# A gate sum moved from the first feed-forward into the mixer of a float32 decoder trunk

## The chip, the cores and the metric

The kernel runs on one core of a Trainium2 chip. TensorE (PE) multiplies matrices, VectorE (DVE) and ScalarE (ACT) work on tiles in on-chip memory, GpSimd (POOL) does little here, and SyncE (SP) issues nearly all transfers from HBM. The engines run beside one another and each takes its own instructions in program order. The metric is the device time of one execution in microseconds (us); "step" below always means one step of the adaLN sums described further on.

## The reference, cut to what matters

Two layers, each made of three sub-layers: a half-step SwiGLU feed-forward, a mixer of three attention branches, and another half-step feed-forward. Every sub-layer has a shift, a scale and a gate, each 1024 wide, that come from the conditioning vector `c`:

```python
mod = (jax.nn.silu(c) @ w_ada[l] + b_ada[l]).reshape(Bn, 3, 3, D_MODEL)
def pre(xx, j):
    return rmsnorm(xx, norm_gain[l, j]) * (1 + mod[:, j, 1]) + mod[:, j, 0]
h = pre(x, 0); x = x + 0.5 * mod[:, 0, 2] * swiglu(h, gate[l, 0], up[l, 0], down[l, 0])
h = pre(x, 1); x = x + mod[:, 1, 2] * (merged(h) @ w_out[l])
h = pre(x, 2); x = x + 0.5 * mod[:, 2, 2] * swiglu(h, gate[l, 1], up[l, 1], down[l, 1])
```

The batch is 1, there are 256 tokens of width 1024, the feed-forward is 2816 wide, and everything is float32. `w_ada` holds 9216 columns per layer, 75 MB in all. The shift and scale of a sub-layer are needed at its norm; its gate is needed only at its end, when the residual is added.

## The kernel before

The sub-layers are numbered s = 0 to 5; s = 1 and s = 4 are mixers. Weights stream through in units of 128 x 1024 numbers. A load (`raw`, 1 MB, three buffers, `load_raws`) holds two units. `feed` (lines 137 to 160) splits each unit into a high part wH (a cast on ScalarE, line 149) and a low part wL (a subtraction on VectorE, line 157), up to five units ahead of the products, with six slots. TensorE then makes three products for each pair of blocks: high with high, low with high, high with low. `step` (line 564) handles one unit: `feed`, `ada_tick`, the unit's products, then whatever follows them.

The adaLN sums run beside this. A sum (s, kind), kind 0 for shift, 1 for scale, 2 for gate, takes eight steps, one for each block of 128 rows of `w_ada`. A step loads 128 x 1024 numbers (512 KB, tag `ada`, two buffers, `ada_load`, line 255), multiplies them by 128 numbers of silu(c) and adds them to the sum's tile `acc` (three buffers). The first step of a sum (kb 0) is on ScalarE (line 280), the other seven on VectorE (line 282). The load of step i + 2 is issued on SP when step i has freed its buffer. Steps go in one fixed order: (0, 2), (1, 0), (1, 1), (1, 2), (2, 0) and so on; steps 16 to 23 are the gate of s = 0, steps 40 to 47 the gate of s = 1.

When a sum is complete, `ada_reduce` (line 326) adds its 128 partitions on TensorE. For a gate that is a product of ones with `acc` in two halves (line 343, tile `adag`, four instructions) and two additions of the bias on VectorE (line 348). For a shift or scale it is a product (line 352, tile `adam`), a copy, transposes and a small evacuation. The dictionary `filler` (line 179) names the sums that are reduced in the gap after a sub-layer, while the next norm runs; every other sum is put on the list `soon` when its eighth step is issued and is reduced five ticks later.

The pace of the steps is set by hand. In `run` (from line 1291) each sub-layer gets the number `need` of steps that are due by its end, plus `SPARE`; `need` is spread over its ticks in proportion to `PACE[s]`. For s = 0 there are 50 ticks left at that point: 8, 8 and 16 gate and up units and 18 of the 22 down units. For s = 1 the parts are 6 value units (pace 0), 14 query and key units, branches of 10, 10 and 12 units, and 4 of the 8 output units. `ada_tick` adds the pace to a credit and issues a step for each whole 1 in it.

`run_rows` (line 703) ends a sub-layer. The body multiplies one unit of 128 rows at a time for all 256 tokens. The last four units (`TAIL`) go piece by piece instead: all four for the first tokens' first 512 columns, then for the next piece, so that residual, norm and transposes (line 487, tile `psn`) of the first tokens run beside the rest. After s = 0 `v_early` (line 938) puts the first value products of the mixer into the gap.

In the mixer (`run_mixer`) the attention stages are placed by hand behind certain units (dictionary `when`): for example the stick-breaking sums (tile `pc`, line 984) behind query unit 9, which need `e` from VectorE (line 978), and the transposes of the second dilated group (tile `pt_dil`, line 1100) behind unit 6 of the first branch, which need that group's scaled probabilities from VectorE (line 1081).

Of the kernel before, what the change touches and what calls it, by code (L numbers as in the profile page):

```python
# [28 lines left out]

# slots of split units, how many of them are split ahead, and slots of loads  # L30
NB = 6
AHEAD = 5
RAWS = 3
# units at the end of a sub-layer whose products go piece by piece, and those that the first norm's transposes follow
TAIL = 4
LEAD = 1
HALVES = ((0, 512), (512, 512))
# columns of the sums that the last rows' products take at a time, by token block
PIECES = (HALVES, ((0, 512), (512, 256), (768, 256)))
# the first shift and scale, by quarter after the first: row blocks on the vector engine, the pass that the rest follows  # L40
FIRST_DVE = (2, 3, 3)
HOOK = (0, 1, 1)
# reductions before the last tokens' transposes, by sub-layer; the others follow
N1 = (1, 3, 3, 2, 1, 0)
# steps of adaLN: how they spread over the parts of each sub-layer, steps beyond what is due, units until a reduction
START_PACE = 0.3
PACE = ((1, 0.75, 1, 1.5), (0, 1.5, 1.5, 1, 0.75, 0.75), (2, 1.5, 1, 1), (1, 0.5, 1, 0.75), (1, 2, 0, 0, 1, 2),
        (1, 1, 1, 1))
SPARE = 1
SOON = 5  # L50
# the last rows' columns on the vector engine; the activation engine takes the others
CUT = 640
# [10 lines left out]
def shape_constants():  # L63
    """One-hot of the bucket of each distance, and the mask of each head by distance (distance 255 - index)."""
    dist = 255 - np.arange(NDIST)
    ok = dist >= 0
    b = _buckets()
    onehot = np.zeros((32, NDIST), np.float32)
    onehot[b[dist[ok]], np.arange(NDIST)[ok]] = 1.0
    mask = np.full((NHEAD, NDIST), NEG, np.float32)  # L70
    for h in range(NHEAD):
        if h < 6:
            w, d = ((128, 1), (512, 4), (2048, 16))[h // 2]
            keep = ok & (dist % d == 0) & (dist // d <= w // d)
        else:
            keep = ok & (dist <= 127)
        mask[h, keep] = 0.0
    return onehot, mask


class Unit:
    """A piece of a weight: `view` picks it from the raw tile of load `raw`; `pe` runs its products."""

# [5 lines left out]
class Trunk:  # L89
# [22 lines left out]

    # ---------------------------------------------------------------- weight stream
    def add_raw(self, loads, small=False):
# [22 lines left out]
    def feed(self, ahead=AHEAD, high=0):  # L137
        """Split the units that lie up to `ahead` in front of the products, H one step before L."""
        self.load_raws()
# [24 lines left out]

    # ---------------------------------------------------------------- adaLN
    def ada_setup(self):
        first = [(0, 0), (0, 1)]
        rest = [(0, 2), (1, 0), (1, 1)]
        for s in range(1, 6):
            rest += [(s, 2)] + ([(s + 1, 0), (s + 1, 1)] if s < 5 else [])  # L170
        self.ada_order = first + rest
        self.ada_pos = 0
        self.ada_kb = 0
        self.ada_acc = {}
        self.ada_raw = []
        self.ada_loaded = 16
        self.gate = {}
        # after which sub-layer a sum is reduced, while the next norm runs; the others as they are complete
        self.filler = {(1, 2): 0, (2, 2): 1, (3, 0): 1, (3, 1): 1, (3, 2): 2, (4, 0): 2, (4, 1): 2, (4, 2): 3,
                       (5, 0): 3, (5, 2): 4}  # L180
        self.credit = 0.0
        self.pace, self.ticks = [0.0], 0
        self.soon = []

    def first_load(self, q):
        """Two blocks of columns of the first shift and scale, into what the feed-forward takes later."""
        t = self.sp.tile([P, KB, 2, 256], F32, tag=("bigA", "bigB")[q % 2], name=f"first{q}", bufs=1)
        for kb in range(KB):
            src = self.a["w_ada"][0, kb * P:(kb + 1) * P, 0:2 * D].rearrange("p (c n) -> p c n", c=2)
            self.nc.sync.dma_start(t[:, kb], src[:, :, 256 * q:256 * q + 256])  # L190
        self.first_src[q] = t

    def first_mac(self, q, kbs):
        """Products of some blocks of rows with the vector, on the vector engine."""
        for kb in kbs:
# [8 lines left out]
    def first_sum(self, q, kbs, acc=False):  # L204
        """Sums over the rows, of products made here or before: a column tile each for the two blocks of the shift
        and of the scale."""
        for kb in ([None] if acc else []) + list(kbs):
# [21 lines left out]
    def first_h(self, q, xt, out):  # L229
        """The first norm's output, two blocks of features."""  # L230
        for i in range(2):
# [94 lines left out]
    def ada_reduce(self, ch):  # L326
        """Sums over the partitions on the tensor engine; returns what is left to do.

        A gate is wanted along the free dimension: ones times the products. Shift and scale are wanted along the
        partitions: four column tiles sum a quarter of the columns each, and transposes turn the rows."""  # L330
        nc = self.nc
# [37 lines left out]

    # ---------------------------------------------------------------- constants  # L370
    def constants(self):
# [67 lines left out]

    # ---------------------------------------------------------------- norm  # L440
    def square(self, t, cols, tag):
        """Mean square over some of the columns."""
        nc = self.nc
# [36 lines left out]
    def norm_pe(self, t, s, xn):  # L480
        """Features to the partitions, one half of them a bank."""
        ps = []
# [8 lines left out]
    def norm_evac(self, t, s, ps, between=()):  # L491
        """Scale and shift by feature, one engine a bank; the high parts too."""
        nc = self.nc
# [46 lines left out]
    def final_gain(self, t, sl):  # L540
        """x times the gain, while the mean square is summed."""
        self.o[t] = self.o.get(t) or self.work([P, D], f"o{t}")
# [19 lines left out]

    # ---------------------------------------------------------------- unit lists
    def step(self, u):
# [15 lines left out]
    def aform(self, u, out, xh, xl, off=0, part="all"):  # L580
        """out += W^T x for one block of 128 columns of the unit; the products with the low part of x come last."""
        nc = self.nc
# [8 lines left out]
    def col_raw(self, src, widths=((0, 256),)):  # L591
        """Load of columns of a [1024, n] weight as [128, 8, 256]."""
        loads = []
# [7 lines left out]
    def plan_ffn(self, l, i, s):  # L601
# [5 lines left out]
        def start_pe(b0, q):  # L607
            """Two blocks of columns over two of rows; both sums of a block share a bank."""
            def pe(u, between=None):
# [74 lines left out]
    def plan_rows(self, w, nk):  # L684
        """Units of one block of 128 rows of a [n, 1024] weight, two a load."""
        us = []
# [9 lines left out]
    def bform(self, u, kb, t, cols, out, xh, xl, first, last):  # L696
        """out += x[t]^T W for one block of rows and some of the columns."""
        sl = slice(t * P, (t + 1) * P)
# [4 lines left out]
    def run_rows(self, us, s, xh, xl, early=None):  # L703
        """Row units to token-major sums, the residual and the next norm.

        The last units' products go piece by piece, so that the norm of the first tokens runs beside them."""
        n = len(us)
# [101 lines left out]

    # ---------------------------------------------------------------- mixer  # L810
    def plan_mixer(self, l, s):
# [125 lines left out]
    def v_early(self, plan):  # L937
        """The first tokens' products with the value columns that are split by now."""
        s = plan["s"]
# [8 lines left out]
    def sb_stages(self, s):  # L948
        """Two heads at a time, keys on the partitions."""
        nc = self.nc  # L950
# [60 lines left out]
    def soft_stages(self, s, l):  # L1011
# [92 lines left out]
        def pv(o, cols, pairs):  # L1104
            """Heads of both halves of the partitions beside one another."""
            n = len(pairs)
# [83 lines left out]
    def run(self):  # L1190
# [100 lines left out]
        for n, plan in enumerate(plans):  # L1291
            s = plan["s"]
            # enough steps of the coming sums for what this sub-layer and the gap behind it reduce
            due = [i for i, (j, kind) in enumerate(self.ada_order)
                   if self.filler.get((j, kind), j - (kind < 2)) <= s]
            need = 8 * (max(due) + 1) - self.ada_pos + SPARE
            if plan["kind"] == "mix":
# [45 lines left out]
```

## Time and profile before

| what | value |
|---|---|
| median of 3 runs | 1215.85 us (1215.71 to 1215.98) |
| profiled execution, span from first to last instruction | 1213.2 us |
| TensorE busy | 1184.2 us, 98% of the span |
| VectorE busy | 830.4 us, 68% |
| ScalarE busy | 615.6 us, 51% |
| transfers | 287.58 MB, mean 237 GB/s |
| mean granted TensorE clock | 0.994 |

The profile tells the span of one execution; the device time has a little more around it, 2.65 us here against the median. The page's share of busy time is a mean over stages that have different limits, so what counts is who ends each wait, stage by stage. Times in the rows are us from the start of the span. In a timeline row the first number is the start, the second the duration, and a bracket tells how long the engine sat idle before it and what released it.

### The profile page before, as it was taken

To read this page: it belongs to the slowest core of one execution; us is meant where nothing else is said; L and a number is where in the kernel's file an instruction comes from. 1 tells how busy PE (TensorE), PEld (TensorE's weight loads), DVE (VectorE), ACT (ScalarE), POOL (GpSimd) and SP (SyncE) were. 2 spreads that over 40 slices of the span, in tenths; PEclk is the share of its full clock that TensorE was granted. 3 is DMA by queue.
4 is the path that set the end of the run, shared out by engine and by line. 5 is a ranking of instruction groups with operands and counts; after the bars stand their busy time and mean duration, and the time that the engine had idled before them with its cause. 6 is when DMAs were issued, how large, how long until landed. Compare 5 with 4: busy or idle time off the path is not lost.

```text
span 1213.2 us, 21570 instructions
## 1 busy us (share of the span) xinstructions
PE 1184.2 (98%) x9005; PEld 1115.3 (92%) x9005; DVE 830.4 (68%) x1075; ACT 615.6 (51%) x953; POOL 17.5 (1%) x38
## 2 busy tenths in 40 slices
PE   6999999899999999999999999999999999999997
PEld 5999987799999999999889999889999998999986
DVE  3677576777889897766577667557766788555544
ACT  5555343546564475444365444346655446444432
POOL 1000000000000000000000000000000000000000
PEclk9999999899999999999999999999999999999999
DMA  9999999698779859877739776758843584656550
GB/s 318 308 307 328 266 328 321 205 299 286 249 241 312 310 186 330 253 243 249 251 112 300 217 243 226 257 157 282 269 153 114 180 273 149 199 184 198 174 173 35
DMA packets 189673, 287.58 MB, mean 237 GB/s; under 512 B 6806, under 2 KB 155496, under 8 KB 189576
## 3 DMA queue, kind: packets, MB, share of 16 engines
q1 hardware_dynamic: 187656, 279.88, 69.7%
q0 software_dynamic: 1776, 6.14, 1.8%
q8 instruction: 70, 1.15, 0.4%
q14 instruction: 27, 0.22, 0.1%
q10 hardware_dynamic: 144, 0.20, 0.0%
HBM read 285.12 MB, written 3.42 MB: 238 GB/s over the span
## 4 chain that ended last, share of the span: by engine, by line
PE 85%; DMA 6%; DVE 4%; issue 2%; ACT 2%; POOL 0%; SPq 0%; POOLq 0%; ACTq 0%; DVEq 0%
PE pf L589 36%; PE pd L701 18%; PE pg L589 11%; PE pq L589 7%; DMA ada<-in_w_ada 5%; PE pf L619 3%; PE pb L589 3%; PE pv L934 2%; DVE acc L282 1%; DVE wL L157 1%; PE psn L487 1%; PE adag L343 1%; DMA first<-in_w_ada 1%; DMA raw<-in_w_ffn_gate 0%; ACT wH L149 0%
## 5 line engine op out<-in xcount | busy, mean ns | idle before, releaser
L157 DVE TENSOR_TENSOR wL<-raw,wH 128x1024 fp32r<-128x1024 f32 (+1 forms) x384 | 461.9, 1211 | 223.2 <-ACT wH L149 222.8
L149 ACT CAST wH<-raw 128x1024 fp32r<-128x1024 f32 (+1 forms) x384 | 393.1, 1041 | 243.9 <-PE pd L701 94.7
L589 PE MATMUL pf<-hH,wH 128*128 128x256 f32 x1312 | 323.0, 284 | 0.4 <-DVE hH L504 0.4
L589 PE MATMUL pf<-hH,wL 128*128 128x256 f32 x1312 | 322.0, 283 | 0.0
L589 PEld LDWEIGHTS pf<-hH,wH 128*128 128x128 f32 x1312 | 251.8, 192 | 1.7 <-issue 0.9
L589 PEld LDWEIGHTS pf<-hH,wL 128*128 128x128 f32 x1312 | 251.8, 192 | 0.2 <-issue 0.2
L589 PE MATMUL pf<-hL,wH 128*128 128x256 f32 x1312 | 183.7, 283 | 0.0
L282 DVE SCALAR_TENSOR_TENSOR acc<-ada,sc,acc 128x1024 f32<-128x1024 f32 x112 | 143.4, 1280 | 43.6 <-DMA ada<-in_w_ada 43.5
L589 PEld LDWEIGHTS pf<-hL,wH 128*128 128x128 f32 x1312 | 169.0, 192 | 0.0
L701 PE MATMUL pd<-wL,ffH 128*128 128x512 f32 (+1 forms) x440 | 154.6, 351 | 3.5 <-DVE wL L157 3.5
L701 PE MATMUL pd<-wH,ffH 128*128 128x512 f32 (+1 forms) x440 | 154.6, 351 | 0.0
L701 PE MATMUL pd<-wH,ffL 128*128 128x512 f32 (+1 forms) x440 | 153.6, 349 | 0.0
L701 PEld LDWEIGHTS pd<-wL,ffH 128*128 128x128 f32 x440 | 83.8, 191 | 15.3 <-DVE wL L157 4.7
L589 PE MATMUL pg<-hH,wH 128*128 128x256 f32 x384 | 96.0, 288 | 0.0
L701 PEld LDWEIGHTS pd<-wH,ffH 128*128 128x128 f32 x440 | 84.0, 191 | 12.2 <-issue 0.8
L589 PE MATMUL pg<-hH,wL 128*128 128x256 f32 x384 | 94.0, 283 | 0.0
L701 PEld LDWEIGHTS pd<-wH,ffL 128*128 128x128 f32 x440 | 83.6, 190 | 11.0
L647 ACT ACTIVATE sil<-pf 128x256 f32<-128x256 f32 x88 | 33.4, 383 | 96.6 <-PE pf L589 96.6
L589 PEld LDWEIGHTS pg<-hH,wH 128*128 128x128 f32 x384 | 73.4, 191 | 2.3 <-issue 1.3
L589 PEld LDWEIGHTS pg<-hH,wL 128*128 128x128 f32 x384 | 73.4, 191 | 0.0
L648 DVE TENSOR_TENSOR f<-pf,sil 128x256 f32<-128x256 f32 x88 | 36.9, 422 | 32.9 <-ACT sil L647 32.9
L589 PE MATMUL pq<-hH,wH 128*128 128x256 f32 x224 | 55.8, 287 | 0.0
(204 smaller groups left out, 1390.5 us busy)
## 6 DMA issues: line engine op xcount, KB each, us to landing
ada<-in_w_ada SPq DMA_DIRECT2D x128, 512.0 KB, 5.6
raw<-in_w_ffn_down SPq DMA_DIRECT2D x44, 1024.0 KB, 5.0
raw<-in_w_in SPq DMA_DIRECT2D x42, 1024.0 KB, 6.6
raw<-in_w_ffn_gate SPq DMA_DIRECT2D x41, 1024.0 KB, 6.7
raw<-in_w_ffn_up SPq DMA_DIRECT2D x41, 1024.0 KB, 6.0
first<-in_w_ada SPq DMA_DIRECT2D x32, 256.0 KB, 6.0
raw<-in_w_out SPq DMA_DIRECT2D x8, 1024.0 KB, 6.9
raw<-in_w_ffn_gate SPq DMA_DIRECT2D x12, 256.0 KB, 6.0
```

The costliest lines, as they stand in the source:

```text
L149: nc.scalar.copy(u.H, u.view(self.raw_tiles[u.raw]))
L157: nc.vector.tensor_tensor(u.L, u.view(self.raw_tiles[u.raw]), u.H, op=ALU.subtract)
L282: self.nc.vector.scalar_tensor_tensor(acc, src, sc, acc, ALU.mult, ALU.add)
L343: nc.tensor.matmul(ps[h], self.ones, acc[:, h * 512:(h + 1) * 512], start=True, stop=True)
L487: self.nc.tensor.transpose(p[:, i * P:(i + 1) * P], xn[:, fb * P:(fb + 1) * P], self.ident)
L589: nc.tensor.matmul(out, w[:, kb, cs], x[:, kb, :], start=i == 0, stop=i == n - 1)
L619: self.nc.tensor.matmul(ps[fb][:, S * up:S * up + S], w[:, 2 * k + up, b * P:(b + 1) * P], x[:, 2 * q + k, :], start=q == 0 and not up and ...
L647: nc.scalar.activation(sil, p[:, :S], AF.Silu)
L648: nc.vector.tensor_tensor(f32, p[:, S:], sil, op=ALU.mult)
L701: self.nc.tensor.matmul(out, x[:, kb, sl], w[:, 0, hs], start=first and i == 0, stop=last and i == 2)
L934: self.nc.tensor.matmul(out, x[:, 4 * (i % 2) + k, sl], w[:, k, :], start=i % 2 == 0 and j == 0, stop=i % 2 == 1 and j == n - 1)
```

## The change

The gate of the second sub-layer, (1, 2), is taken out of `filler`. Its steps are then due by the end of s = 1 and not of s = 0, and it is reduced from the list `soon`, in the middle of the mixer, and not in the gap after s = 0. `SPARE` becomes a number for each sub-layer, 5 for s = 0, so that five of the gate's eight steps still belong to s = 0. `PACE[0]` becomes even. The rest of the diff takes away comments and docstrings.

```diff
-PACE = ((1, 0.75, 1, 1.5), (0, 1.5, 1.5, 1, 0.75, 0.75), (2, 1.5, 1, 1), (1, 0.5, 1, 0.75), (1, 2, 0, 0, 1, 2),
+PACE = ((1, 1, 1, 1), (0, 1.5, 1.5, 1, 0.75, 0.75), (2, 1.5, 1, 1), (1, 0.5, 1, 0.75), (1, 2, 0, 0, 1, 2),
         (1, 1, 1, 1))
-SPARE = 1
+SPARE = (5, 1, 1, 1, 1, 1)
...
-        self.filler = {(1, 2): 0, (2, 2): 1, (3, 0): 1, (3, 1): 1, (3, 2): 2, (4, 0): 2, (4, 1): 2, (4, 2): 3,
+
+        self.filler = {(2, 2): 1, (3, 0): 1, (3, 1): 1, (3, 2): 2, (4, 0): 2, (4, 1): 2, (4, 2): 3,
                        (5, 0): 3, (5, 2): 4}
...
             due = [i for i, (j, kind) in enumerate(self.ada_order)
                    if self.filler.get((j, kind), j - (kind < 2)) <= s]
-            need = 8 * (max(due) + 1) - self.ada_pos + SPARE
+            need = 8 * (max(due) + 1) - self.ada_pos + SPARE[s]
```

## Rows read from the trace of the kernel before

**Rows 1.** The page, part 1: busy time, share of the span, instructions.
```profile
PE 1184.2 (98%) x9005; PEld 1115.3 (92%) x9005; DVE 830.4 (68%) x1075; ACT 615.6 (51%) x953; POOL 17.5 (1%) x38
```
**Rows 2.** Waits of TensorE: line, releaser, total us, times, longest.
```profile
PE pd L701 <- DVE wL L157: 3.5, 2, 2.6
```
**Rows 3.** Busy time by stretch: us, PE, PEld, DVE, ACT, POOL, clock, DMA share, GB/s.
```profile
161.00:209.00 48.00, 48.00 (x269) 40.54 (x268) 32.24 (x32) 19.66 (x22) 0.00 (x0) 1.00 0.93 330
```
**Rows 4.** Timeline of TensorE, end of s = 0: start, duration, instruction, idle before.
```profile
204.70 0.40 PE L701 MATMUL pd<-wH,ffH 128*128 128x512 f32 x1
...
207.48 0.40 PE L701 MATMUL pd<-wH,ffH 128*128 128x512 f32 x1
...
211.85 0.53 PE L701 MATMUL pd<-wL,ffH 128*128 128x512 f32 x1 [2.59 <-DVE wL L157]
...
219.03 0.40 PE L701 MATMUL pd<-wH,ffH 128*128 128x512 f32 x1
...
226.44 1.27 PE L487 MATMUL psn<-ident,xn 128*128 128x128 f32 x8 [2.04 <-ACT xn L474]
...
228.62 1.88 PE L343 MATMUL adag<-acc,ones 128*128 128x512 f32 x4
```
**Rows 5.** Timeline of TensorE, the same end in s = 2.
```profile
608.88 0.40 PE L701 MATMUL pd<-wH,ffH 128*128 128x512 f32 x1
...
620.80 1.88 PE L343 MATMUL adag<-acc,ones 128*128 128x512 f32 x4
```
**Rows 6.** The chain that ended last, 150 to 240: start, us, what.
```profile
201.58 7.78 DMA ada<-in_w_ada
...
211.72 1.29 DVE acc L282
...
228.78 1.72 PE adag L343 x4
```
**Rows 7.** Instructions of the tiles acc, adag, ada: ns min/median/max; us to landing.
```profile
L282 DVE SCALAR_TENSOR_TENSOR acc<-ada,sc,acc x112: 1274/1279/1287, 78.7 to 997.5; 128x1024 f32<-128x1024 f32 x112
L348 DVE TENSOR_TENSOR gate<-adag,gate x12: 679/682/687, 122.1 to 1025.5; 128x512 f32<-128x512 f32 x12
DMA to landing us min/median/max: 3.5/5.6/19.3
```
**Rows 8.** Waits of VectorE, first from 161 to 222, then from 254 to 345.
```profile
DVE acc L282 <- DMA ada<-in_w_ada: 12.4, 8, 2.5
...
DVE acc L282 <- DMA ada<-in_w_ada: 12.0, 8, 3.2
```
**Rows 9.** Timeline of VectorE in the first mixer.
```profile
255.08 1.28 DVE L282 SCALAR_TENSOR_TENSOR acc<-ada,sc,acc 128x1024 f32<-128x1024 f32 x1
...
277.23 1.28 DVE L282 SCALAR_TENSOR_TENSOR acc<-ada,sc,acc 128x1024 f32<-128x1024 f32 x1 [2.38 <-DMA ada<-in_w_ada]
...
279.57 0.95 DVE L978 SCALAR_TENSOR_TENSOR e<-z,e 128x768 f32<-128x768 f32 x1
...
283.55 1.28 DVE L282 SCALAR_TENSOR_TENSOR acc<-ada,sc,acc 128x1024 f32<-128x1024 f32 x1 [0.83 <-DMA ada<-in_w_ada]
...
322.85 1.28 DVE L282 SCALAR_TENSOR_TENSOR acc<-ada,sc,acc 128x1024 f32<-128x1024 f32 x1
...
325.44 1.14 DVE L1081 TENSOR_SCALAR p_dil<-p_dil,sm_dil 128x768 f32<-128x768 f32 x2
```
**Rows 10.** Timeline of TensorE in the first mixer.
```profile
281.81 0.59 PE L984 MATMUL pc<-e,tri 128*128 128x256 f32 x2
...
319.89 0.64 PE L352 MATMUL adam<-acc,ones 128*32 128x256 f32 x8
...
326.73 1.18 PE L1100 MATMUL pt_dil<-ident,p_dil 128*128 128x128 f32 x9 [0.25 <-DVE p_dil L1081]
```
**Rows 11.** Busy time by stretch, as in Rows 3, two stretches of 2 us.
```profile
216.00:218.00 2.00, 2.00 (x6) 1.57 (x5) 1.66 (x2) 0.44 (x1) 0.00 (x0) 0.50 0.87 258
224.00:226.00 2.00, 0.40 (x4) 0.20 (x2) 1.67 (x4) 0.71 (x3) 1.10 (x2) 1.00 0.96 330
```

## The prediction

> **What bounds the kernel now.** I read the page first, then TensorE's waits, then the stages around the change, last the order of VectorE's queue. TensorE is busy for 98% of the span [rows 1], so a change can win only where TensorE waits or runs at half clock. Its largest wait late enough to be touched is for the low parts of weights in the tail of s = 0, 3.5 us in two waits [rows 2]. Before that tail it never stops from 161 to 209, while the transfers run at 330 GB/s [rows 3]. The chain of waits through that stage is a ring: load of a step, product, load, product [rows 6]. Each product sits in VectorE's queue in front of weight splits, and VectorE waited 12.4 us for such loads from 161 to 222 [rows 8].
>
> The price of the stall: from the first product of the tail to the gate's reduction there are 21.14 us in s = 0 (207.48 to 228.62) [rows 4] and 11.92 us in s = 2 (608.88 to 620.80), where the same products never wait [rows 5]. The difference is 9.2 us: 3.5 for weights, 2.0 before the transposes because the residual came late, and the rest mostly half clock: at 216 to 218 the granted clock is 0.50 [rows 11], which is 1.2 GHz, and the first product of full pace is that of 219.03 [rows 4].
>
> **The steps.** In s = 0 `need` falls from 33 to 29 and the pace becomes 0.58 everywhere; over the 18 down units it was 0.868, so 15.6 steps become 10.4. Fifty times 0.58 adds up to a hair under 29, so 28 steps are issued and s = 1 starts at step 44. There `need` is 88 - 44 + 1 = 45 instead of 40, and the pace on query, key and first-branch units rises from 1.034 to 1.164 a unit. By unit 4 of the first branch 22 steps are issued instead of 19. From s = 2 on the schedules are the same.
>
> **The ring** can do one step in half of (5.6 to land + 1.28 for the product [rows 7] + 0.08 to issue), 3.48 us. A down unit takes 2.78 us (204.70 to 207.48 [rows 4]), so the down stage asked for one step in 3.2 us, more than the ring gives, and will ask for one in 4.8.
>
> **Part 1, tail of s = 0: -9.2.** With the ring no longer full, VectorE reaches the splits early; working its queue from 164 on with these durations, the splits catch up with the free slots by down unit 10, and the four tail units, wanted within 3 us of one another, are ready. I take the whole 9.2; the other end is 5.6, if only the idle time goes and the clock still falls.
>
> **Part 2, the gap: 0.** The reduction leaves the gap (1.72 us [rows 6]), but there TensorE waits anyway, first for the high part of the new activations, then for the last tokens' norm, which hangs on the residual of the last piece. Nothing is gained; up to 1.7 us of idle time appears.
>
> **Part 3, the reduction in the mixer: +1.7.** It comes at query unit 8, in a stretch without idle time: 1.72 us [rows 6]. Its two additions on VectorE, 1.2 us [rows 7], wait for TensorE, and behind them in the queue stand step 53, the next split and the stick-breaking work. Eight PSUM banks go round; the two moved tiles find theirs free. The bias load on SP moves with step 40 and delays nothing.
>
> **Part 4, the fuller ring in the mixer: +8.9.** The attention stages give VectorE little room: the stick-breaking `e` ends at 280.5, 1.3 us before TensorE asks [rows 9, 10], and the scaled probabilities of the second dilated group come 0.25 too late already [rows 10]. The nineteen steps 49 to 67 lie between 255.08 and 322.85 [rows 9], 3.77 us each; VectorE waited 12.0 us for their loads [rows 8]. Now 22 steps must pass before the same scaling. I work VectorE's queue on by its own order: each step begins when VectorE is free and 5.6 + 0.08 us after the step two before it ended. Applied to the kernel before, this ends the scaling at 326.3; the row says 326.5 [rows 9]. For the changed kernel, in times of before: steps 44 to 51 start as the loads of 49 to 56 allowed, with two steps at query unit 6; step 52 lands at 283.55, as step 57 did [rows 9], but it now stands in front of `e`, which starts at 284.75 instead of 279.57. TensorE, itself 1.7 later, waits 2.2 there. Steps 55, 57, 58 and 65 wait for loads again (295.9, 302.8, 305.05, 333.2), and the scaling ends at 336.85. TensorE starts the transposes 9.9 later than at 326.98, after some 7 us of idle time; 0.7 us of a scale's reduction that stood ahead of them [rows 10] comes behind. So 10.6 later in all, 1.7 of it from part 3. No later wait appears after that. The bounds: 0, if VectorE's waits take up all the new work; 11.8, if each of the three extra steps costs 3.77 and the additions 1.2, less 0.7 that TensorE is late itself. The value is near the upper end because the ring's own rows give it.
>
> The Trainium skill, "DMA: Bandwidth & Descriptors", section "Anatomy of one DMA — SWDGE (gpsimd) path", gives about 2.0 us plus bytes / 436e3 for a transfer, an estimate of 3.2 us for a step's load. By that the ring would do a step in 2.3 us, part 4 would be near 0, and the first rival below would be the outcome. The trace does not agree: the median landing of these loads is 5.6 us [rows 7], with the weights' loads on the same engines.
>
> **Part 5, the clock: +3.4.** 2.6 us of idle time at 211.85, with 0.95 more behind it, was followed by half clock until 219.0, about 7 us of it [rows 4, 11]; 2.04 us at 226.44 was not [rows 4, 11]. A wait of some 7 us should bring the half clock back, and half of 6.8 us is lost. The bounds are 0 and 3.6.
>
> **Sum** on the profiled span: 1213.2 - 9.2 + 1.7 + 8.9 + 3.4 = 1218.0; the runs lie 2.65 above the span, so 1220.6.
>
> **The rivals.**
> First, the ring keeps up: landings in the mixer get short enough (under some 4.5 us) for VectorE's idle 12 us to hide the added steps. Then only parts 1 and 3 count: 1208.4, up to 1211 with one wait left. For it: the transfers are not full in the mixer. Against it: eight waits for these loads there. This is the case that is not slower. 0.22.
> Second, the ring binds but the idle time is spread over several attention stages, and the clock stays: 1217.2. 0.20.
> Third, half of part 4 and no half clock: 1212.8. 0.10.
> Fourth, the tail of s = 0 keeps its half clock and ends only 5.6 earlier, while the ring binds in the mixer: 1224.2. The change then does not do in s = 0 what it is meant to. 0.06.
>
> **How the numbers follow.** The forecast, 1220.6, has 0.42, its own range is 1218.3 to 1223. A difference of 0.2%, 2.4 us, is about what a measurement of this kernel can tell from no change. Faster: 0.22 and most of the third rival, 0.28. Same: the second and the rest of the third, 0.24. Slower: 0.48. For 8 in 10 the range runs from 1209.0 to 1223.0: it leaves out the best of the first rival and the fourth.
>
> **What would show it.** Part 1: no wait for wL in the tail of s = 0, clock 1.00 there, 11.9 us from the tail's first product to the end of its last. Part 2: up to 1.7 us of idle time before the early value products. Part 3: four instructions of `adag` at query unit 8. Part 4: waits of `pc` for `e` and of `pt_dil` for `p_dil`, several us, and steps 3.5 us apart. Part 5: clock 0.5 behind the long wait. The prediction is wrong if the mixer's waits stay under 2 us, or if the tail still waits.

## The result, and the profile after

The changed kernel is slower: median 1226.49 us against 1215.78 us in four executions of each, a ratio of 1.0079 (95% interval 1.0061 to 1.0097; the quotient of the two medians is 1.0088). Its executions took 1220.45, 1226.0, 1226.99 and 1227.32 us. The traced one is the shortest, with a span of 1218.7 us. The forecast, 1220.6, fits that execution and not the other three, which lie above the range's end of 1223.0. So two things are to be explained: where the traced execution loses, and what the others lose on top.

First the traced execution. The page, part 1, answers [rows 1]: the work is the same, and TensorE's share falls by a point.

```profile
PE 1183.1 (97%) x9005; PEld 1114.7 (91%) x9005; DVE 830.9 (68%) x1075; ACT 616.6 (51%) x953; POOL 17.2 (1%) x38
```

TensorE's waits (releaser, total us, times, longest) answer [rows 2]:

```profile
PE pt_dil L1100 <- DVE p_dil L1081: 5.1, 1, 5.1
PE pc L984 <- DVE e L978: 2.7, 1, 2.7
...
PE adam L358 <- ACT acc L354: 2.0, 1, 2.0
...
PE pv L934 <- ACT hH L518: 1.2, 1, 1.2
```

The 3.5 us for wL are gone, and there are two waits in the mixer's attention, as forecast. The third line was not forecast: in s = 0 the transposes of the shift sum (1, 0) wait for ScalarE's copy. TensorE's timeline (start, duration, instruction, idle before) places them and answers [rows 4, 10]:

```profile
163.78 0.44 PE L358 MATMUL adam<-ident,acc 128*128 128x128 f32 x2 [1.98 <-ACT acc L354]
...
209.53 0.40 PE L701 MATMUL pd<-wH,ffH 128*128 128x512 f32 x1
...
219.51 1.04 PE L487 MATMUL psn<-ident,xn 128*128 128x128 f32 x8
...
268.55 1.98 PE L343 MATMUL adag<-acc,ones 128*128 128x512 f32 x4
...
278.98 1.19 PE L984 MATMUL pc<-e,tri 128*128 128x256 f32 x2 [2.71 <-DVE e L978]
...
329.24 2.18 PE L1100 MATMUL pt_dil<-ident,p_dil 128*128 128x128 f32 x9 [5.12 <-DVE p_dil L1081]
...
431.13 1.04 PE L487 MATMUL psn<-ident,xn 128*128 128x128 f32 x8
```

The first transposes of the norm, psn, come at 219.51 instead of 226.44: s = 0 ends 6.9 us earlier. The tail itself is 9.0 us shorter: from its first product (209.53, before 207.48) to these transposes there are 9.98 us, before 18.96. But it starts 2.05 later, by the wait that was not forecast. The same transposes behind the mixer come at 431.13; in the kernel before they stand at 425.14:

```profile
425.14 1.04 PE L487 MATMUL psn<-ident,xn 128*128 128x128 f32 x8
```

The mixer, from one to the other, takes 211.6 us instead of 198.7. These two numbers, the end of s = 0 and the length of the mixer, are given for every run below.

Busy time by stretch (columns as in [rows 3]) answers [rows 3, 11]:

```profile
161.00:209.00 48.00, 46.02 (x255) 39.28 (x254) 34.00 (x34) 20.64 (x22) 0.00 (x0) 1.00 0.94 332
216.00:218.00 2.00, 2.00 (x12) 1.69 (x11) 0.76 (x3) 0.72 (x2) 0.40 (x2) 1.00 0.22 75
280.00:284.00 4.00, 4.00 (x27) 3.82 (x26) 3.92 (x5) 3.94 (x6) 0.00 (x0) 0.78 0.56 182
328.00:330.00 2.00, 0.76 (x4) 0.76 (x5) 1.97 (x4) 0.00 (x0) 0.00 (x0) 0.50 0.63 236
```

The tail of s = 0 runs at full clock (1.00, before 0.50), and half clock has come to the mixer, behind both of its waits (0.78 at 280 to 284, 0.50 at 328 to 330). VectorE's waits for step loads, first from 161 to 222 and then from 254 to 345, answer [rows 8] (12.4 and 12.0 before), and its timeline answers [rows 9]:

```profile
DVE acc L282 <- DMA ada<-in_w_ada: 3.2, 3, 1.8
...
DVE acc L282 <- DMA ada<-in_w_ada: 14.2, 7, 4.8
```

```profile
276.68 1.29 DVE L282 SCALAR_TENSOR_TENSOR acc<-ada,sc,acc 128x1024 f32<-128x1024 f32 x1 [3.43 <-DMA ada<-in_w_ada]
277.88 0.95 DVE L978 SCALAR_TENSOR_TENSOR e<-z,e 128x768 f32<-128x768 f32 x1
...
325.46 1.28 DVE L282 SCALAR_TENSOR_TENSOR acc<-ada,sc,acc 128x1024 f32<-128x1024 f32 x1 [4.76 <-DMA ada<-in_w_ada]
...
328.05 1.14 DVE L1081 TENSOR_SCALAR p_dil<-p_dil,sm_dil 128x768 f32<-128x768 f32 x2
```

In both places a product that waits for its load stands directly in front of what TensorE waits for. The wait has moved with the steps: out of the tail of s = 0, into the attention.

### The profile page after: what moved, and what is told of

It is laid out like the page before. It is cut to its first block, busy times and chain, and to the rows that moved or that the text cites. A ratio compares the mean times of both kernels' runs of the same rounds, so it can differ in the third digit from the quotient of the medians.

```text
span 1218.7 us, 21563 instructions
## 1 busy us (share of the span) xinstructions
PE 1183.1 (97%) x9005; PEld 1114.7 (91%) x9005; DVE 830.9 (68%) x1075; ACT 616.6 (51%) x953; POOL 17.2 (1%) x38
## 4 chain that ended last, share of the span: by engine, by line
PE 81%; DMA 7%; DVE 5%; ACT 3%; issue 2%; POOL 0%; POOLq 0%; SPq 0%; ACTq 0%; DVEq 0%
PE pf L589 37%; PE pd L701 22%; PE pg L589 9%; DMA ada<-in_w_ada 4%; PE pq L589 3%; PE pb L589 2%; PE pf L619 2%; DVE acc L282 2%; PE pv L934 1%; DVE wL L157 1%; DMA first<-in_w_ada 1%; ACT wH L149 1%; DMA raw<-in_w_ffn_down 1%; DMA raw<-in_w_in 1%; PE adag L343 1%
```

## The experiments

Psn is the start of the first transposes after s = 0 in the traced execution, the mixer's length is as above, and the time is the median of all timed executions. The ratio is to runs of the kernel before on the same chip. Four chips were used, one for e1 to e4, one for e5 to e8, one for e9 to e11 and one for e12; the medians of the kernel before on them were 1215.64, 1215.96, 1217.15 and 1216.31 us. There is one trace for each kernel, and it need not be that of a middling execution: the one of e6 took 3.8 us more than its median, the one of e2 3.6.

| kernel | time, us | ratio (95%) | psn | mixer |
|---|---|---|---|---|
| before | 1215.85 | 1 | 226.4 | 198.7 |
| changed | 1226.49 | 1.0079 (1.0061 to 1.0097) | 219.5 | 211.6 |
| e1_again | 1227.36 | 1.0094 (1.0072 to 1.0116) | 224.9 | 217.7 |
| e2_reduce_only | 1216.76 | 1.0014 (1.0001 to 1.0027) | 229.7 | 201.0 |
| e3_spread_only | 1218.48 | 1.0017 (1.0002 to 1.0031) | 228.6 | 198.3 |
| e4_no_load | 1213.15 | 0.9979 (0.9969 to 0.9989) | 222.3 | 200.3 |
| e5_turn_later | 1222.83 | 1.0047 (1.0033 to 1.0060) | 218.2 | 214.8 |
| e6_mixer_37 | 1213.62 | 0.9977 (0.9966 to 0.9988) | 225.6 | 199.1 |
| e7_both | 1208.20 | 0.9931 (0.9915 to 0.9946) | 217.4 | 199.2 |
| e8_extra_bytes | 1227.50 | 1.0087 (1.0066 to 1.0107) | 223.7 | 212.7 |
| e9_before_sum_moved | 1216.68 | 0.9999 (0.9987 to 1.0011) | 227.9 | 199.4 |
| e10_third_buffer | 1207.16 | 0.9925 (0.9908 to 0.9942) | 218.0 | 200.2 |
| e11_four_work_tiles | 1229.12 | 1.0102 (1.0084 to 1.0120) | 224.4 | 212.4 |
| e12_before_third_buffer | 1204.56 | 0.9904 (0.9890 to 0.9917) | 217.3 | 198.0 |

The theory after the result: a product in VectorE's queue waits for its load, two buffers set how soon that comes, and whatever stands behind it is late. The rivals: the moved reduction itself, the sum of bytes in s = 0, VectorE's own added work.

**e1_again, the changed kernel once more.** No edit, so as to have a trace of one of the longer executions.

> The changed kernel unchanged. Its one traced execution took 1220.45 us (span 1218.7), three others 1226.0 to 1227.3; the trace of one of those is wanted. Theory A (the loads' landing times differ from execution to execution, and the mixer now hangs on them): most runs near 1226 again; in a trace with a span near 1224 TensorE's rows agree with those of 1218.7 until about 255 (first psn transposes at 219.5, first pv at 222.8), and the 6 us are added between 255 and 345, as longer waits of pc for e and pt_dil for p_dil (2.7 and 5.1 us before) or as more stretches with a granted clock of 0.50. Rival B (the tail of s = 0 falls back into its stall in those executions): psn at 223 to 226.5, a wait of pd for wL of 2 to 3.5 us, and the mixer as in the trace of 1218.7. Rival C (it lies behind 345): rows agree, shifted by 6 us, up to 345, and part from one another later.

Measured: 1223.15 to 1231.93 us; the traced execution is the longest. TensorE's waits, two stretches, and the timelines of VectorE and of ScalarE ahead of the third wait:

```profile
PE pt_dil L1100 <- DVE p_dil L1081: 7.2, 1, 7.2
...
PE pc L984 <- DVE e L978: 5.2, 1, 5.2
PE adam L358 <- ACT acc L354: 3.8, 1, 3.8
```

```profile
168.00:172.00 4.00, 4.00 (x14) 3.18 (x13) 4.00 (x5) 1.49 (x2) 0.00 (x0) 0.57 0.91 312
...
336.00:340.00 4.00, 0.15 (x1) 0.15 (x2) 3.90 (x7) 0.00 (x0) 0.00 (x0) 0.50 0.99 338
```

```profile
148.19 1.28 DVE L282 SCALAR_TENSOR_TENSOR acc<-ada,sc,acc 128x1024 f32<-128x1024 f32 x1 [12.49 <-DMA ada<-in_w_ada]
...
165.51 0.42 DVE L648 TENSOR_TENSOR f<-pf,sil 128x256 f32<-128x256 f32 x1
```

```profile
165.97 0.40 ACT L651 CAST ffH<-f 128x256 fp32r<-128x256 f32 x1 [2.46 <-DVE f L648]
166.28 1.04 ACT L149 CAST wH<-raw 128x1024 fp32r<-128x1024 f32 x1
167.22 0.36 ACT L354 COPY acc<-adam 128x256 f32<-128x256 f32 x1
```

Neither A nor B alone is right. Psn is 5.4 later than in the first trace, with no wait for wL: all three waits are longer, and now the one in s = 0 brings half clock too (0.57). The mixer adds 6.1 (217.7 against 211.6). Together that is 11.5, the whole difference of the two spans (1230.2 and 1218.7). The rows name the chain in s = 0: VectorE waited 12.49 us for one step load and works off its splits late; the last up block's `f` comes at 165.51, ScalarE's cast waits 2.46 for it, and behind the cast, in ScalarE's order, stands the copy that the transposes want. In the seven traces with this schedule of s = 0 and these transposes at down unit 2 (the run with three load buffers among them, with 0.45) the wait was 1.98, 3.78, 3.43, 3.66, 3.96, 3.12 and 0.45; the five between 3.1 and 4.0 were all followed by half clock, the other two were not. The first trace had the mildest case with two buffers.

The trace shows one more thing. The load that VectorE waits 12.49 us for was issued at 125.68 and took 22.5 us to land, the longest of the trace. It ran beside a transfer of 2.3 MB on POOL's queue. POOL's timeline, that transfer's size and landing, and the landings of step loads issued from 60 to 165:

```profile
121.57 1.11 POOL L432 DMA_DIRECT2D scr<-row  x1 [5.39 <-DMA row<-mk]
...
scr<-row POOLq DMA_DIRECT2D x1, 2298.0 KB, 24.2
...
DMA to landing us min/median/max: 3.5/7.2/22.5
```

In every trace, of either kernel, the longest landing (15.9 to 23.4 us) is that of a step load issued while this transfer was under way. With two buffers and this schedule of s = 0, VectorE's wait for it goes roughly with the wait at the copy: 9.05 and 1.98 us in the first trace, 10.34 and 3.12 in e11, 10.65 and 3.43 in e4, 11.70 and 3.96 in e8, 12.49 and 3.78 here, 13.15 and 3.66 in e6. With three buffers VectorE doesn't wait there. So the stall in s = 0 starts from one long landing, and two buffers let it through; that POOL's transfer is what makes the landing long wasn't tried. In the mixer the load in front of `e` took 5.6 us to land in the first trace and 7.9 here.

**e2_reduce_only: the reduction in the mixer, the steps as before.** The changed kernel with the old `PACE[0]` and

```diff
-SPARE = (5, 1, 1, 1, 1, 1)
+SPARE = (9, 1, 1, 1, 1, 1)
...
-            self.soon.append([SOON, ch])
+            self.soon.append([SOON + 11 if ch == (1, 2) else SOON, ch])
```

> The gate is reduced at query unit 8 of the mixer, as in the changed kernel, but the pace of s = 0 and the 33 steps of it stay as in the kernel before, so that the mixer has its 40 steps. Theory A (the extra steps, not the reduction, cost the mixer its time): the tail of s = 0 stalls as before (psn near 226.4, half clock at 216), the mixer gets 1.7 us for the four adag instructions, no wait of pc for e over 0.5 us, and pt_dil waits under 1 us; 1216 to 1218 us. Rival D (the reduction's two additions of 0.68 us on VectorE, or its place between units, throw the attention's order out by themselves): pt_dil waits 1.5 to 4 us, 1219 to 1223 us.

Measured: 1216.76 us, a ratio of 1.0014; the tail stalls as before (psn at 229.7 in a long execution), the mixer is 2.3 longer, and neither pc nor pt_dil waits. Theory A holds: the reduction costs about its 1.7 us, no more.

**e3_spread_only: the even pace alone, the gate still in the gap.**

```diff
-PACE = ((1, 0.75, 1, 1.5), (0, 1.5, 1.5, 1, 0.75, 0.75),
+PACE = ((1, 1, 1, 1), (0, 1.5, 1.5, 1, 0.75, 0.75),
```

> The kernel before with an even pace in s = 0 alone: 33 steps at 0.66 a unit, the gate reduced in the gap, 40 steps left for the mixer. A down unit of 2.78 us then asks for a step in 4.2 us, which is more than the 3.48 us that the two buffers need. Theory A (the tail's stall comes from the ring alone): no wait for wL, clock 1.00 in the tail, first psn some 7 to 9 us earlier than 226.4, the mixer's rows as before but shifted; 1206.5 to 1209 us. Rival E (fewer steps in s = 0 are needed, 28 and not 33): the wait for wL stays at 1.5 us or more, half clock behind it, 1212 to 1216 us.

Measured: 1218.48 us, psn at 228.6. Both expectations miss. The tail is clean, with no wait for wL, but the time was lost before it. TensorE's timeline, and the landing of step loads from 60 to 165:

```profile
145.83 0.39 PE L589 MATMUL pf<-hH,wL 128*128 128x256 f32 x1 [1.78 <-DVE wL L157]
...
152.26 0.96 PE L352 MATMUL adam<-acc,ones 128*32 128x256 f32 x8 [3.41 <-DVE acc L282]
...
163.10 0.69 PE L358 MATMUL adam<-ident,acc 128*128 128x128 f32 x2 [2.77 <-ACT acc L354]
```

```profile
DMA to landing us min/median/max: 3.5/7.9/15.9
```

In the gate and up units a step load takes 7.9 us to land, not 5.6, so two buffers give a step in (7.9 + 1.28 + 0.08) / 2 = 4.6 us there. A unit is 24 products, 85 or 86 of which pass in 10 us, so 2.8 us, and 0.66 a unit asks for a step every 4.2. The number 3.48 on which my expectation stood is a median over the whole kernel; this stage has its own. The median alone doesn't place the stall, though: all three waits come behind the step loads issued from 124.95 to 144.34, beside POOL's transfer, which took 8.7 to 15.9 us to land. What the even pace does without them wasn't tried. Spreading the steps evenly moved the stall from the down units into the gate and up units.

**e4_no_load: no loads for steps 44 to 67.**

```diff
+            if 44 <= i < 68:
+                t = self.x[:, 0, :]
+            else:
+                t = self.sp.tile([P, D], F32, tag="ada", name=f"ada{i}", bufs=2)
+                self.nc.sync.dma_start(t, self.ada_src(i))
```

> The changed kernel, but steps 44 to 67 take their 128 x 1024 numbers from the residual tile in on-chip memory instead of a load (those sums are wrong by that; VectorE's work stays). Theory A (the ring of two load buffers binds in the mixer): VectorE has no waits for loads from 254 to 320, pc waits for e and pt_dil for p_dil under 0.7 us each, no half clock from 281 to 345; 1207 to 1211 us, the tail's gain and the reduction's 1.7 us alone. Rival F (VectorE's own work for three more steps in front of e and of the scaling, 3.84 us, binds): these waits stay at 1.5 to 4 us in all; 1213 to 1219 us.

Measured: 1213.15 us, the mixer 200.3 instead of 211.6 to 217.7. VectorE does the same work; pc and pt_dil don't wait, and the clock is 1.00 from 281 to 345. Theory A holds in the mixer: the loads cost it all but the reduction. The time is 2 above the expectation because of s = 0, where these waits of TensorE remain:

```profile
PE adam L361 <- ACT acc L357: 3.4, 1, 3.4
...
PE pt_swa L1103 <- DVE p_swa L1091: 1.0, 1, 1.0
```

**e5_turn_later: the transposes of (1, 0) four units behind the product.**

```diff
-                        self.soon.append([2, x[1], left])
+                        self.soon.append([4 if x[1] == (1, 0) else 2, x[1], left])
```

> The changed kernel with one number changed: the transposes of the sum (1, 0) come four units behind its product instead of two, at down unit 4 instead of 2. In the traces so far they waited 2.0, 3.8 and 3.4 us there for ScalarE's copy, which stands behind the last gate and up block's work. Theory A (the copy's place in ScalarE's queue is the cause): no wait of adam for acc over 0.5 us and clock 1.00 from 160 to 180, and nothing takes its place: the first psn comes 2 to 6 us earlier than in the repeated run of the changed kernel (224.9), near 219 to 221; 1221 to 1225 us against 1227.4. Rival H (the weights are late there anyway, because the transfers are full): the same time reappears as waits for raw loads, wL or wH in the down stage, psn at 222 to 225; 1226 to 1229 us.

Measured: 1222.83 us, 4.5 less than 1227.36 (e8_extra_bytes, on the same chip, took 1227.50). TensorE's timeline:

```profile
218.24 1.03 PE L487 MATMUL psn<-ident,xn 128*128 128x128 f32 x8
...
279.02 1.19 PE L984 MATMUL pc<-e,tri 128*128 128x256 f32 x2 [4.02 <-DVE e L978]
...
330.31 2.18 PE L1100 MATMUL pt_dil<-ident,p_dil 128*128 128x128 f32 x9 [4.88 <-DVE p_dil L1081]
```

The wait is gone, nothing has taken its place, and psn comes at 218.2. The mixer's waits stay. Theory A holds.

**e6_mixer_37 and e7_both: eight steps out of the mixer.** The scale (3, 1) is summed by the end of s = 2:

```diff
-        self.filler = {(2, 2): 1, (3, 0): 1, (3, 1): 1, (3, 2): 2,
+        self.filler = {(2, 2): 1, (3, 0): 1, (3, 2): 2,
```

e7_both has this, the edit of e5_turn_later, and `PACE[2] = (1, 1, 1, 1)`.

> The changed kernel with the scale sum (3, 1) taken out of the gap after s = 1: its eight steps are then due in s = 2, and the first mixer gets 37 steps instead of 45 (0.957 a unit on query, key and first-branch units). Theory A (it is the number of step loads before the attention's deadlines that costs the mixer its 12 us): pc waits for e and pt_dil for p_dil under 1 us, no half clock from 270 to 350, and the time that of the run without loads, 1213.2, plus up to 2: 1212 to 1215.5 us. Rival I (the gate's reduction, which now falls at query unit 9, right in front of e and pc, makes its own wait): pc waits 1 to 2.5 us, 1215.5 to 1220 us. Rival J (s = 2 pays for its added steps and for the reduction of 1.1 us outside a gap): a new wait between 430 and 480, 1216 to 1222 us.

> Both edits together, the transposes of (1, 0) at down unit 4 and the scale (3, 1) in s = 2, and an even pace in s = 2. Theory A: neither adam in s = 0 nor pc and pt_dil in the mixer wait 1 us, no half clock from 150 to 350; 1208 to 1212 us, faster than the kernel before by 0.3 to 0.6%. Rival H (the transfers are full in s = 0 anyway): the tail or the down stage takes back 2 to 4 us; 1212 to 1216 us.

Measured: 1213.62 us with a mixer of 199.1, and 1208.20 us with psn at 217.4 and a mixer of 199.2. Neither pc nor pt_dil waits. The number of steps in front of the attention is what cost the mixer its time, and by e4_no_load it is their loads (theory A in both). For e7_both the stretch from 150 to 350 has TensorE busy for 197.55 of 200 us at full clock:

```profile
150.00:350.00 200.00, 197.55 (x1441) 181.45 (x1440) 156.78 (x207) 111.93 (x180) 2.39 (x4) 1.00 0.79 270
```

So the change's gain in s = 0 is real, and without its two new stalls the kernel is faster than before.

**e9_before_sum_moved: the edits of s = 2 on the kernel before.**

> The kernel before, not the changed one, with the two edits of s = 2 alone: the scale (3, 1) out of the gap after s = 1, and an even pace in s = 2. Its first mixer gets 32 steps instead of 40. Theory A (these edits only take the price of the change away; the 7.8 us that both together gained come from s = 0): the tail of s = 0 stalls as in the kernel before (psn near 226 to 229, half clock near 212 to 220), the mixer had no stall to lose, and the time stays at that of the kernel before, within 2 us: 1214 to 1218 us. Rival L (the lighter mixer or s = 2 gains by itself, so that the gate's move is not what made the combination faster): 1208 to 1212 us.

Measured: 1216.68 us, a ratio of 0.9999, with the tail's stall in place. These edits gain nothing alone; they only take away what the change cost the mixer. Theory A.

**e8_extra_bytes: five transfers of 512 KB that nobody waits for.**

```diff
+        if i in (34, 36, 38, 40, 42):
+            dum = self.dp.tile([P, D], F32, tag=f"dum{i}", name=f"dum{i}")
+            self.nc.sync.dma_start(dum, self.ada_src(i))
```

> The changed kernel with five added transfers of 512 KB in the down stage of s = 0, from HBM to HBM, issued on SP behind steps 34, 36, 38, 40 and 42. They use no buffer and nobody waits for them: the bytes of the five steps that the change moved out, without their place in the ring and without VectorE's work. Theory A (the ring of two buffers is what the tail of s = 0 hung on): the step loads land a little later, psn moves by 0 to 2.5 us against the changed kernel (224.9 in the repeated run), no wait for wL; 1227 to 1230 us. Theory K (the transfers of s = 0 are full, some 310 GB/s from 60 to 205, and what the tail hung on is the sum of bytes: five steps are 2.6 MB, 8.2 us): the tail's stall is back, pd waits for wL or wH 2 us or more, half clock near 215 to 225, psn at 228 to 234; 1231 to 1238 us.

Measured: 1227.50 us, as the changed kernel without them. The stretch of the down units:

```profile
150.00:205.00 55.00, 50.64 (x288) 43.19 (x288) 41.10 (x41) 24.80 (x31) 0.00 (x0) 0.97 0.96 357
```

The transfers move 357 GB/s there; e1_again moved 327. The step loads land later, in 6.9 us by the median of this stretch against 5.0 in e1_again and 6.0 in the first trace, but the bytes find room: psn is at 223.7, and no wait for wL appears. Theory K falls: a DMA share of 0.93 [rows 3] was not a full pipe.

**e11_four_work_tiles, e10_third_buffer, e12_before_third_buffer: the two buffers.** Four work tiles make room; e11 has that alone, e10 the third load buffer with it, e12 both on the kernel before.

```diff
-    def work(self, shape, name, tag="w", bufs=5, dtype=F32):
+    def work(self, shape, name, tag="w", bufs=4, dtype=F32):
...
-        while self.ada_loaded < 8 * len(self.ada_order) and len(self.ada_raw) < 2:
+        while self.ada_loaded < 8 * len(self.ada_order) and len(self.ada_raw) < 3:
...
-            t = self.sp.tile([P, D], F32, tag="ada", name=f"ada{i}", bufs=2)
+            t = self.sp.tile([P, D], F32, tag="ada", name=f"ada{i}", bufs=3)
...
-        x4 = [self.sp.tile([P, 4, S], F32, tag="ada", name=f"xt{q}", bufs=2) for q in range(2)]
+        x4 = [self.sp.tile([P, 4, S], F32, tag="ada", name=f"xt{q}", bufs=3) for q in range(2)]
```

> The changed kernel with four work tiles instead of five and two load buffers as before: what the room for the third buffer costs by itself. If the work tiles are not short: 1225 to 1229 us, as the changed kernel. If they are: a new wait of PE or DVE in the gaps between sub-layers or in the attention stages, up to 1240 us.

> The changed kernel with a third load buffer for the steps; to make room, the work tiles of 4.5 KB go from five to four. To be compared with the run that has four work tiles and two load buffers. Theory A (two buffers in turn, each held for landing plus product, set the pace of the steps in the mixer): three of them give a step in 2.3 us instead of 3.5; VectorE's wait for loads between 254 and 345 falls from some 12 us to under 5, pc and pt_dil wait under 1 us, no half clock from 270 to 350; 8 to 14 us faster than the run with two. Rival M (the transfers themselves give no more: with three loads under way each lands later): the median landing in the mixer rises from 5.3 to over 7 us, the waits stay over 2 us each, within 4 us of the run with two.

> The kernel before, with the same third load buffer and four work tiles as the run before. Theory A (the two buffers, by VectorE's queue, made the stall in the tail of s = 0 too, and the place of the gate's sum is not what counts): no wait of pd for wL, clock 1.00 from 205 to 225, first psn at 217 to 219 as in the changed kernel with three buffers (218.0), and the time within 2 us of that one, 1206 to 1209 us. Rival N (0.87 steps a down unit are too many for s = 0 whatever the buffers, by VectorE's own work or by the sum of bytes): a wait for wL or raw loads of 1.5 us or more stays in the tail, psn at 221 to 227; 1210 to 1216 us.

Measured: 1229.12, 1207.16 and 1204.56 us. The third buffer takes 22 us from the changed kernel, more than I expected, because it also removes the wait in s = 0 (0.45 us are left). For e12 I expected 1206 to 1209; it is faster than that. VectorE's wait for loads from 254 to 345 in e11, then in e10, and the landing of step loads from 230 to 350 in e10:

```profile
DVE acc L282 <- DMA ada<-in_w_ada: 16.0, 8, 4.9
```

```profile
DVE acc L282 <- DMA ada<-in_w_ada: 4.3, 5, 1.1
```

```profile
DMA to landing us min/median/max: 3.6/5.8/8.5
```

With three loads under way each lands about as fast as with two (5.8 against 5.3 in the changed kernel and 5.1 in e11): rival M falls, and the ring of two is shown to be the cause. With it gone, the kernel before is the better one. TensorE's timeline at the end of s = 0, first e12, then e10:

```profile
217.33 1.04 PE L487 MATMUL psn<-ident,xn 128*128 128x128 f32 x8
...
219.28 1.88 PE L343 MATMUL adag<-acc,ones 128*128 128x512 f32 x4
220.65 0.62 PE L934 MATMUL pv<-wH,hH 128*128 128x256 f32 x1
```

```profile
221.32 0.39 PE L934 MATMUL pv<-wH,hH 128*128 128x256 f32 x1 [1.22 <-ACT hH L518]
```

In e12 the reduction fills the gap in which e10 waits 1.22 us, and the mixer is 2.2 shorter (198.0 against 200.2). No wait for wL is left with 0.87 steps a down unit: theory A, rival N falls. What remains of the change would be its own price, 2.6 us by the medians. That is hardly clear of noise: the two ran on different chips, and their intervals (0.9908 to 0.9942 and 0.9890 to 0.9917) overlap a little.

## Why the prediction was right and wrong

**Part 1, -9.2.** The mechanism was right: no wait for wL, the tail at 1.00, VectorE's waits for loads down from 12.4 to 3.2, and the tail itself 9.0 us shorter. The step that failed is "I take the whole 9.2" for the end of s = 0: in the traced execution it comes 6.9 earlier, in the others with this schedule, two buffers and the transposes at unit 2, 0.8 (225.6) to 4.1 (222.3). I followed the steps that the new pace moves, not the reduction that moves with them: (1, 0) goes from down unit 2 to down unit 0, where ScalarE still has the last gate and up block's work in front of its copy. With the transposes two units later, psn is at 218.2 and 217.4 (e5_turn_later, e7_both), 8.2 and 9.1 earlier than before. So the 9.2 was there, and one new wait, which the prediction puts at nothing, took some 2 us of it back in the first trace (219.5 against 217.4) and some 7 in e1_again (224.9), half clock included.

**Part 2, 0.** Right: 1.21 us of idle time before the early value products.

**Part 3, +1.7.** Right: four instructions at query unit 8, 1.98 us as the row shows them, and e2_reduce_only comes to 1.1 us by the medians on its chip (its ratio of 1.0014 makes 1.7) with a mixer that is 2.3 longer.

**Part 4, +8.9, and part 5, +3.4.** With part 3 the forecast for the mixer was +14.0; the traced execution has +12.9, the other traces with its schedule and two buffers 212.4 (+13.7), 212.7 (+14.0), 214.8 (+16.1) and 217.7 (+19.0). Working VectorE's queue by hand held: `e` was to start at 284.75 in times of before and the scaling to end at 336.85; after, plus the 7.4 by which the mixer's first query product comes earlier (243.53 against 250.94), they stand at 285.3 and 336.6. One reading in it was off: the row of pt_dil gives its start as 326.73, with the wait of 0.25 already over, so that "9.9 later than at 326.98" should be some 0.25 more, which changes nothing. What it left out is that the landing times it was fed with differ from execution to execution (the load in front of `e`: 5.6 us in the first trace, 7.9 in e1_again, with waits at pc of 2.7 and 5.2), and that the shorter wait, at pc, brings half clock too (0.78 at 280 to 284). The Trainium skill's estimate (DMA: Bandwidth & Descriptors, "Anatomy of one DMA — SWDGE (gpsimd) path"), by which the ring would have kept up, is further off in the gate and up units, where the landing is 7 to 8 us by the median, than in the mixer. That section is about transfers issued from GpSimd, while these loads are issued on SP; no run here shows one of them on the other path.

**The sum and the range.** For the traced execution the sum came out at 1218.0 of span against 1218.7, partly by luck: 2.3 too much in part 1 stood against 1.1 too much in the mixer and shifts of half a microsecond outside. That 1220.6 also meets its time, 1220.45, is luck for another 0.9: an execution takes 1.7 us more than its own span (1220.45 against 1218.7), and the 2.65 that I added holds the 0.9 by which the traced execution of before was shorter than the median. For the median the forecast was 6 too low, and that stands in part 1: the traced executions nearest to it, of e8_extra_bytes (1226.28) and e11_four_work_tiles (1227.41), have mixers of 212.7 and 212.4, as parts 3 to 5 say (198.7 + 14.0), but their psn comes at 223.7 and 224.4 where part 1 gives 217.2. The range failed because I took one execution of before, stable within 0.3 us over its runs, as the measure of how sure a time is; in later runs the kernel before itself lay between 1212.9 and 1220.8. A wait that hangs on landing times, and half clock that sets in behind some lengths of it and not behind others, makes a spread of 9 us (1223.15 to 1231.93). The nearest rival was the fourth (1224.2, 0.06), right that s = 0 keeps a stall, wrong about which: it is at the start of the down units, not in the tail. That the first rival, the ring keeps up, gives 1208.4 agrees with the run with a third buffer, 1207.16.

## What to carry to other kernels

When a pace is changed, follow all that is counted in its ticks: here a reduction that slid two units ahead took back 2 to 7 of the 9 us that the removed wait gained. Where a stall comes from a ring of buffers, try a ring one deeper before moving its load: here that was worth more than the move. The landing time that decides is that of the stage, not the median of the kernel, and a single long landing can start the stall. If a wait hangs on landing times, the forecast's range needs the spread of several executions, and the working with the longest landings beside the median.

The Trainium skill, Perfetto Trace Analysis, "Optimization Strategy", says that a gap which keeps coming back on the engine that should be saturated can mean too few buffers. The trace agrees on the cause, but the gaps stood on VectorE (eight waits, 12.0 us [rows 8]), while TensorE was busy throughout.

## What the runs showed of the hardware

- Three step loads under way land in a median of 5.8 us in the mixer, two in 5.3 (the changed kernel). Five added transfers of 512 KB from 150 to 205 raised the rate from 327 to 357 GB/s and cost no time, though the step loads there landed in 6.9 us by the median instead of 5.0.
- A step load's landing differs by stage: 6.9 to 7.9 us by the median from 60 to 165, against 4.4 to 5.8 in the mixer (fourteen traces). In that stretch a transfer of 2.3 MB on POOL's queue is under way for 20.7 to 25.3 us. The longest landing of each trace, 15.9 to 23.4 us, is of a step load issued beside it; of those issued from 60 to 116 none took more than 9.9. In e1_again the rate from 121.6 to 145.8 is 239 GB/s at a DMA share of 0.97, from 110 to 120 it is 318 at 0.96. That this transfer is what delays the loads wasn't tried.
- Idle times of TensorE from 2.6 to 7.2 us in s = 0 and the mixer were each followed by a stretch of 4 us with a granted clock under 0.8. At 2 us it goes both ways: after 1.98 (the changed kernel) and 2.04 (before) it stayed at 1.00, after 1.97 in e9_before_sum_moved, shortly behind another half-clock stretch, it was 0.58 at 228 to 232.
